# Three more seven-product couples in the down projections of a two-layer encoder kernel

## The chip, the cores and the metric

The kernel runs on one core of a Trainium2 chip. The metric is the device time of one launch in microseconds. Times of whole launches are medians over several runs. A profile is one execution of the program, recorded by the hardware profiler. TensorE (PE) multiplies, VectorE (DVE) and ScalarE (ACT) do the elementwise work, GpSimd (POOL) helps and issues some transfers, and SyncE (SP) issues most transfers to the DMA engines.

## What is computed

The reference is a trunk of two layers on a sequence of 256 tokens with 2048 features, in float32. Each layer adds a token mixer (bidirectional mLSTM in layer 0, bidirectional HGRN2 in layer 1) and then a convolutional gated MLP with 5504 hidden features. The change lies in the MLP, whose part of the reference is:

```python
def conv_glu(hn, w_up, conv_w, conv_b, w_down):
    u = hn @ w_up
    a, v = jnp.split(u, 2, axis=-1)
    s = a.shape[1]
    pad = CONV_W // 2
    ap = jnp.pad(a, ((0, 0), (pad, pad), (0, 0)))
    c = conv_b
    for j in range(CONV_W):
        c = c + ap[:, j:j + s] * conv_w[j]
    return (jax.nn.gelu(c, approximate=False) * v) @ w_down
...
    for layer in range(DEPTH):
        ...
        h = h + mix
        h = h + conv_glu(rmsnorm(h, norm_ffn_g[layer]), ffn_w_up[layer], ffn_conv_w[layer],
                         ffn_conv_b[layer], ffn_w_down[layer])
    return rmsnorm(h, final_g)
```

## The kernel before

**Precision.** Every float32 product is made of three matmuls. An operand is split into a high part, rounded by a copy to fp32r, and a low part, the rest. For weights ScalarE casts the high part `wh` (L147) and VectorE subtracts it from the original to get `wl` (L148). The three products are high by high, high by low and low by high (`product`, L236 issues their matmuls). Weights come from HBM as `raw` tiles, so the chain for each piece is load, cast, subtract, three matmuls.

**Stages.** The work of TensorE is one stream: mLSTM projections and chunks, its out projection, and then the MLP of layer 0; then the same for HGRN2 and the MLP of layer 1. The hidden features of an MLP are handled in two parts, 22 chunks of 128 in part 0 and 21 in part 1. Part 0's *up run* computes 22 chunks of a and v (L357 and L361, tokens on the columns), then its two *down pairs* multiply the 22 chunks into the four column blocks of 512 of the output, two blocks to a pair. Part 1 does the same with 21 chunks. The order of a whole MLP is thus: up run of part 0, two down pairs, up run of part 1, two down pairs.

**Eviction of an up chunk** (`done_up`, from L1197). ScalarE and VectorE add the two halves of the product (L1203, L1204), multiply by the norm's factor (L1206), do the convolution, the gelu and the gate (L1208 to L1212) in a temporary tile `avc`, and split the result into the tile `g` (L1214, L1215), which is the stationary operand of the down pair.

**A down pair** (`squares_by_seven`) takes the hidden chunks two at a time. Such a *couple*, or unit, is a 2 by 2 block product: two halves of the tokens by two hidden chunks, times two hidden chunks by two column blocks. Eight products of blocks do it, or seven in the manner of Strassen and Winograd, if sums of the blocks are there: S1 to S4 of the token blocks, T1 to T4 of the weight blocks. With three matmuls of 512 columns to a product, an ordinary unit has 24 matmuls and a unit by seven has 21. The products go to eight banks of PSUM: P1, P6, P7 and P5, which collect sums over all units by seven, and C11, C12, C21 and C22, which collect for the output blocks directly. After the last unit by seven, `mid` (L585 to L596) adds P1, P6, P7 and P5 into the hidden state `hm`; after the last unit of the pair, `done` (L602) adds the C banks. A following up chunk takes its two banks from the same ring as P1, P6, P7 and P5.

**Token sums** (`token_sums`, L565 to L579) are made during the up run: when the second chunk of a unit by seven is evicted, VectorE forms S1 to S4 (L571) and their splits (L572 to L576). Three of the four go to a new tile `sx`. The fourth is the last argument of the function; it overwrites halves of the tile `g` of the unit's first chunk that a unit by seven doesn't need.

**Weight sums.** Most of the units by seven have their T blocks prepared during an up run or a mixer (`prepare`, L638): the four blocks are loaded, four subtractions are made on VectorE, and the result is stored to a scratch tensor `tscr` in HBM. In the up runs the loads and stores are issued by GpSimd (L399). The down pair then loads a `raw` tile (1536 columns from the weights at L135, 512 from `tscr` at L199) and a `T` tile (1536 columns from `tscr`, L198). The units named in `FLY` make their T blocks on the spot instead (L207).

**Buffers.** `temporary` (L183) gives out the tiles `avc`, `T` and the f tiles. In the MLP they share one ring of three buffers (`TEMP`). Which units go by seven is set by the table `SEVEN`, by layer and part, the same units for both pairs of a part. The order in which instructions stand on each engine is made by a scheduler from the program, and SyncE's loads wait in their order for the buffer that each overwrites.

Of the kernel before, what the change touches and what calls it, by code (L numbers as in the profile page):

```python
# [49 lines left out]
SEVEN = ((1, 2, 3, 4, 5, 6, 7, 8, 9), (1, 2, 3, 4, 5, 6, 7, 8)), ((1, 2, 3, 4, 5, 6, 7, 8, 9), (1, 2, 3, 4, 5, 6, 7))  # L50
# [16 lines left out]
def trunk_kernel(ctx, tc, xT, x_d, fg_d, pp_d, cst_d, w_gate, w_first, w_aq, w_ak, w_av, w_ao, w_aout, w_ao2,  # L67
# [12 lines left out]
    ones = keep.tile([P, T], F32, name="ones")  # L80
# [144 lines left out]
    def squares_by_seven(ch, fetch, ready):  # L225
# [47 lines left out]
        units, last = (ch.nk + 1) // 2, max(ch.seven)  # L273
        for u in range(units):
# [127 lines left out]
    class Norm:  # L402
# [52 lines left out]
        def spread(self):  # L455

            dg = ev.tile([P, T], F32, tag="dg", bufs=1, name="dg")
# [5 lines left out]
            self.R_ = ev.tile([P, T], F32, tag="R", bufs=2, name="R")  # L463
# [233 lines left out]
    def mlstm(norm, nxt):  # L697
# [59 lines left out]
        def gates(gs):  # L757
            with tc.tile_pool(name="gt", bufs=1) as gp:
# [25 lines left out]
                scan(B[f_, 128:256], ones[f_, 128:256], lf[f_, 128:256], 0.0, ALU.mult, ALU.add)  # L784
# [108 lines left out]
        for pr in range(AH // 2):  # L893
# [36 lines left out]
            def done_first(ps, done_v=done_v):  # L930
# [252 lines left out]
    def ffn(layer, norm, nxt):  # L1183
# [13 lines left out]
        def done_up(f, i, GT, SX, seven):  # L1197
            def go(ps):
# [25 lines left out]
        for part, (f0, nf) in enumerate(((0, FA), (FA, FB))):  # L1224
            GT, SX, todo, finished = [], {}, [], []
# [9 lines left out]
            for i in range(nf):  # L1235
                chunks.append(Chunk("fm", w_up[layer, f0 + i], KT, norm.x, done_up(f0 + i, i, GT, SX, SEVEN[layer][part]),
# [17 lines left out]
            seven, fly = SEVEN[layer][part], FLY[2 * layer + part]  # L1254
            n = len(seven) - len(fly)
# [135 lines left out]
```

## Time and profile before

| what | value |
|---|---|
| median of 3 runs | 2366.11 us (2365.32 to 2366.84) |
| the profiled execution | 2365.95 us, with a span of 2364.2 us |
| granted TensorE clock | 1.00 in every MLP stage |
| TensorE busy | 2354.3 us |
| VectorE, ScalarE, GpSimd busy | 1995.5, 1469.7, 297.2 us |
| DMA | 632.98 MB, mean 268 GB/s |
| layer 0: up run 0, down pairs 0, up run 1, down pairs 1 begin at | 389, 634.6, 743.0, 976 us |
| layer 1: the same | 1665, 1910.7, 2018.2, 2251 us |
| layer 1's out projection begins at | 1597 us |

A row of the timeline gives the start in us, the duration, the engine, the line of the kernel, the operation, the output and input tiles, the shape, and in brackets how long the engine had been idle and what ended that. A group row gives the number of instructions, the busy time, the mean in ns of one, and the idle time ahead of them with the releasers. A row of the windows gives for a stretch of time the busy time of each engine, the granted clock, the share of the DMA engines and the rate. SPq is SyncE's queue, whose rows are the issues of transfers.

### The profile page before, as it was taken

The page shows a single profiled execution, that of the slowest core. Times are in us where ns is not written, and L with a number is a line of the kernel's source. Part 1 is how long each engine was busy: PE and PEld are TensorE (multiplying, and loading weights), DVE is VectorE, ACT ScalarE, POOL GpSimd, SP SyncE. Part 2 cuts the span into 40 slices and gives each one's busy share as a digit, 9 for nine tenths or more (in the row PEclk, how much of TensorE's full clock was granted, in tenths as well). Part 3 has the DMA queues.
Part 4 walks back from the last instruction along what each step waited for, and adds up shares of the span by engine and source line. Part 5 has one row for each costly group of instructions (what it writes and reads, how often), then busy time and mean ns, then how long its engine had stood idle before and what let it go on. Part 6 is the DMA issues. An engine that isn't in the chain of part 4 may idle for free.

```text
span 2364.2 us, 38476 instructions
## 1 busy us (share of the span) xinstructions
PE 2354.3 (100%) x14545; PEld 2017.3 (85%) x14545; DVE 1995.5 (84%) x3087; ACT 1469.7 (62%) x2340; POOL 297.2 (13%) x436
## 2 busy tenths in 40 slices
PE   9999999999999999999999999999999999999998
PEld 8888888888888888888888888888888888888887
DVE  7777687889898899897888888778799989899887
ACT  7655456555665555676777777766555566555565
POOL 0100001111000111000232322220011100111100
PEclk9999999999999999999999999999999999999999
DMA  8776656889788898796656666556788888799895
GB/s 302 240 245 244 214 193 217 289 312 320 251 324 320 310 323 317 267 330 227 214 200 224 218 216 213 202 174 235 250 306 318 297 299 330 278 326 328 279 356 201
DMA packets 122267, 632.98 MB, mean 268 GB/s; under 512 B 13776, under 2 KB 14928, under 8 KB 77664
## 3 DMA queue, kind: packets, MB, share of 16 engines
q1 hardware_dynamic: 92736, 525.83, 63.6%
q0 software_dynamic: 28768, 103.89, 12.1%
q8 instruction: 114, 1.87, 0.3%
q10 hardware_dynamic: 576, 0.79, 0.1%
q14 instruction: 73, 0.60, 0.1%
HBM read 562.24 MB, written 68.22 MB: 267 GB/s over the span
## 4 chain that ended last, share of the span: by engine, by line
PE 97%; DVE 1%; DMA 1%; issue 1%; ACT 0%; POOL 0%; SPq 0%; POOLq 0%; DVEq 0%; ACTq 0%
PE mm L357 37%; PE mm L361 19%; PE mm L373 18%; PE pc L236 11%; PE mm L236 7%; DVE wl L148 1%; PE pn L857 1%; PE py L1116 1%; PE pd L1066 0%; PE pa L1066 0%; DMA T<-tscr 0%; PE pz L438 0%; DMA raw<-in_w_first 0%; PE S L843 0%; ACT wh L147 0%
## 5 line engine op out<-in xcount | busy, mean ns | idle before, releaser
L357 PE MATMUL mm<-xt,wh 128*128 128x512 f32 x3776 | 1312.4, 394 | 0.0
L148 DVE TENSOR_TENSOR wl<-raw,wh 128x1024 fp32r<-128x1024 f32 (+1 forms) x844 | 1037.2, 1234 | 245.9 <-ACT wh L147 239.0
L147 ACT CAST wh<-raw 128x1024 fp32r<-128x1024 f32 (+1 forms) x844 | 876.3, 1043 | 545.3 <-PE mm L357 334.6
L361 PE MATMUL mm<-xt,wl 128*128 128x256 f32 x3776 | 1043.6, 278 | 0.0
L357 PEld LDWEIGHTS mm<-xt,wh 128*128 128x128 f32 x3776 | 705.7, 188 | 160.8 <-ACT jk L540 0.4
L361 PEld LDWEIGHTS mm<-xt,wl 128*128 128x128 f32 x3776 | 709.5, 188 | 4.5
L373 PE MATMUL mm<-wh,xt 128*128 128x512 f32 x1024 | 324.9, 393 | 0.5 <-ACT wh L147 0.3
L236 PE MATMUL pc<-wh,g 128*128 128x512 f32 (+1 forms) x716 | 243.2, 388 | 0.0
L373 PEld LDWEIGHTS mm<-wh,xt 128*128 128x128 f32 x1024 | 191.7, 188 | 40.0 <-ACT wh L147 1.0
L373 PE MATMUL mm<-wl,xt 128*128 128x512 f32 x512 | 199.7, 391 | 0.0
L638 DVE TENSOR_TENSOR praw<-praw 128x512 f32<-128x512 f32 x252 | 174.1, 691 | 12.9 <-DMA praw<-in_w_d 7.9
L236 PEld LDWEIGHTS pc<-wh,g 128*128 128x128 f32 x716 | 134.2, 188 | 28.0 <-ACT wh L147 0.4
L236 PE MATMUL mm<-wh,sx 128*128 128x512 f32 x432 | 153.6, 389 | 0.0
L148 DVE TENSOR_TENSOR wl<-T,wh 128x1024 fp32r<-128x1024 f32 (+1 forms) x144 | 136.4, 959 | 16.9 <-ACT wh L147 16.1
L147 ACT CAST wh<-T 128x1024 fp32r<-128x1024 f32 (+1 forms) x144 | 118.8, 834 | 49.4 <-DMA T<-tscr 19.5
L236 PE MATMUL pc<-wl,g 128*128 128x512 f32 (+1 forms) x358 | 138.8, 388 | 0.0
L1203 ACT COPY avc<-mm 128x256 f32<-128x256 f32 x172 | 64.3, 374 | 92.4 <-PE mm L361 92.4
L373 PEld LDWEIGHTS mm<-wl,xt 128*128 128x128 f32 x512 | 96.2, 188 | 18.5
L399 POOL DMA_DIRECT2D tscr<-praw x96 | 51.5, 537 | 468.0 <-DVE praw L638 446.9
L1079 DVE TENSOR_TENSOR QK<-QK,G 128x256 f32<-128x256 f32 x224 | 104.3, 514 | 6.2 <-ACT kq L1058 5.9
L1058 ACT COPY kq<-QK 128x512 f32<-128x512 f32 x112 | 74.4, 669 | 37.5 <-DVE QK L1079 29.6
L236 PEld LDWEIGHTS mm<-wh,sx 128*128 128x128 f32 x432 | 81.1, 188 | 16.8
(248 smaller groups left out, 2325.6 us busy)
## 6 DMA issues: line engine op xcount, KB each, us to landing
raw<-in_w_up SPq DMA_DIRECT2D x172, 1024.0 KB, 6.8
praw<-in_w_d POOLq DMA_DIRECT2D x96, 512.0 KB, 6.5
tscr<-praw POOLq DMA_DIRECT2D x96, 512.0 KB, 6.3
raw<-in_w_bq SPq DMA_DIRECT2D x48, 1024.0 KB, 5.0
T<-tscr SPq DMA_DIRECT2D x63, 768.0 KB, 7.8
raw<-in_w_d SPq DMA_DIRECT2D x60, 768.0 KB, 6.2
raw<-in_w_ao SPq DMA_DIRECT2D x24, 1024.0 KB, 4.9
raw<-in_w_d SPq DMA_DIRECT2D x24, 1024.0 KB, 6.9
```

The source lines that it names most:

```text
L147: pin(act.copy(wh[:, :m], r))
L148: pin(dve.tensor_tensor(wl[:, :m], r, wh[:, :m].bitcast(F32), ALU.subtract))
L236: pin(pe.matmul(ps, a, b, start=bank not in begun, stop=stop and i == 2))
L357: hold(pe.matmul(ps[f], wh[:, c:c + P], x, start=k + kk == 0, stop=False))
L361: hold(pe.matmul(ps[f][:, 0:T], wl[:, c:c + P], x[:, 0:T], start=False, stop=k + kk == ch.nk - 1))
L373: pe.matmul(ps[t], x[:, a + t * P:a + (t + 1) * P], w[:, c], start=st and i == 0, stop=sp and i == 2)
L399: tc.keep_in_program_order(pool.dma_start(dst, src))
L638: hold(dve.tensor_tensor(out, x, y, ALU.subtract))
L857: pe.matmul(pn[:, 0:258], w, v, start=(i == 0), stop=(i == len(parts) - 1))
L1058: act.copy(m, blocks(QK, h))
L1079: dve.tensor_tensor(two[:, j], two[:, j], by[:, j], ALU.mult)
L1203: act.copy(z, p[:, T:2 * T])
```

## The change

The table of units by seven now has one entry for each pair, not one for each part. Unit 10, the last of part 0, goes by seven in the second pair of both layers; it stands directly ahead of the up run of part 1. Unit 8 goes by seven in the first pair of part 1 of layer 1, the last pair but one of the kernel. That makes three more units by seven.

- A unit that goes by seven in one pair of its part only must leave both halves of `g` as they are for the other pair. Its fourth token sum goes to a tile of its own, `sy`.
- If the last unit of a pair goes by seven, its products into P1, P6, P7 and P5 come first, then `mid`, and then those into C12, C11 and C21. C22 gets its last product from the last unit that doesn't go by seven (`alone`).
- Three more units have their T blocks prepared: 12 more transfers on GpSimd's queue, three more T loads and three more loads from `tscr` on SyncE's, and 12 more subtractions at L638.
- To make room, the tile `ones` has 128 columns in place of 256, `dg` takes the buffer of `jk`, `R` has one buffer in place of two, and `gs` moves to a buffer of the MLP's pool.

```diff
-SEVEN = ((1, 2, 3, 4, 5, 6, 7, 8, 9), (1, 2, 3, 4, 5, 6, 7, 8)), ((1, 2, 3, 4, 5, 6, 7, 8, 9), (1, 2, 3, 4, 5, 6, 7))
+SEVEN = (range(1, 10), range(1, 11)), (range(1, 9), range(1, 9)), (range(1, 10), range(1, 11)), (range(1, 9), range(1, 8))
...
-    ones = keep.tile([P, T], F32, name="ones")
+    ones = keep.tile([P, P], F32, name="ones")
...
         units, last = (ch.nk + 1) // 2, max(ch.seven)
+        alone = max(set(range(units)) - set(ch.seven))
...
-                    product(ps, x, w, u == last and ps in psm_)
+                    product(ps, x, w, u == last if ps in psm_ else end)
...
-                products((P1, A11, B11), (C12, S4, B22))
+                products((P1, A11, B11))
+                if not end:
+                    products((C12, S4, B22))
                 T2, T3 = piece()
                 products((P6, S2, T2), (P7, S3, T3))
                 B21, T1 = piece()
-                products((C11, A12, B21), (P5, S1, T1))
+                if not end:
+                    products((C11, A12, B21))
+                products((P5, S1, T1))
                 T4, _ = piece()
-                products((C21, A22, T4))
+                if not end:
+                    products((C21, A22, T4))
                 if u == last:
                     ch.mid(psm_)
                     ch.rest = ch.ends
+                if end:
+                    products((C12, S4, B22), (C11, A12, B21), (C21, A22, T4))
                 continue
...
-                product(ps, y, v, end)
+                product(ps, y, v, end or ps is C22 and u == alone)
...
-            dg = ev.tile([P, T], F32, tag="dg", bufs=1, name="dg")
+            dg = ev.tile([P, 512], F32, tag="jk", bufs=1, name="dg")[:, 0:T]
...
-            self.R_ = ev.tile([P, T], F32, tag="R", bufs=2, name="R")
+            self.R_ = ev.tile([P, T], F32, tag="R", bufs=1, name="R")
...
-                gs = ev.tile([P, T], F32, tag="gs", name="gs")
-                act.copy(gs, pq[:, 0:T])
                 startup.close()
                 begin()
+                gs = box["mp"].tile([P, 768], F32, tag="W", bufs=2, name="gs")[:, 0:T]
+                act.copy(gs, pq[:, 0:T])
...
-                if i % 2 and i // 2 in seven:
-                    n = seven.index(i // 2)
+                if i % 2 and (i // 2 in seven or i // 2 in other):
+                    n = i // 2 - 1
                     z = GT[i - 1][:, P:T], GT[i - 1][:, T + P:2 * T]
+                    if not (i // 2 in seven and i // 2 in other):
+                        y = mp.tile([P, T], F32R, tag="sy", name="sy")
+                        z = y[:, 0:P], y[:, P:T]
                     SX[i // 2] = token_sums(mp, n, box["c"], c, avc[:, 0:2 * T], z)
```

**What moves.** The first place is SyncE's queue at the first pair of part 0 in layer 0. The `raw` tiles are those of units 3 onward (in_w_d0 is the pair's weights), the `T` tiles likewise: T_6409 before and T_6429 after belong to unit 3, T_6451 and T_6471 to unit 4. Before:

```order
162 L135 DMA raw_6407<-in_w_d0 128x1536
163 L199 DMA raw_6407<-tscr 128x512
164 L135 DMA raw_6449<-in_w_d0 128x1536
165 L199 DMA raw_6449<-tscr 128x512
166 L198 DMA T_6409<-tscr 128x1536
167 L135 DMA raw_6491<-in_w_d0 128x1536
168 L199 DMA raw_6491<-tscr 128x512
169 L198 DMA T_6451<-tscr 128x1536
170 L198 DMA T_6493<-tscr 128x1536
```

After, the same stretch of the queue:

```order
162 L135 DMA raw_6427<-in_w_d0 128x1536
163 L199 DMA raw_6427<-tscr 128x512
164 L135 DMA raw_6469<-in_w_d0 128x1536
165 L199 DMA raw_6469<-tscr 128x512
166 L135 DMA raw_6511<-in_w_d0 128x1536
167 L199 DMA raw_6511<-tscr 128x512
168 L198 DMA T_6429<-tscr 128x1536
169 L198 DMA T_6471<-tscr 128x1536
170 L198 DMA T_6513<-tscr 128x1536
```

The T of unit 3 has moved behind the raw tile of unit 5. In the ring of three it takes the buffer that unit 2's T lets go; before it took that of the last up chunk but one.

The second place is VectorE at the border from the second pair of part 0 to the up run of part 1 in layer 1. The hm and u rows are the evacuation of the banks named mm and pc; the wl rows from raw_20706 on (before) and from raw_20771 on (after) belong to the up run. Before:

```order
2446 L589 TENSOR_TENSOR hm_75<-hm_75,mm_20296 128x512
2447 L590 TENSOR_TENSOR u_20715<-u_20715,mm_20297 128x512
2448 L148 TENSOR_TENSOR wl_20697<-raw_20684,wh_20696 128x1024
2449 L591 TENSOR_TENSOR hm_75<-hm_75,mm_20299 128x512
2450 L593 TENSOR_TENSOR hm_75<-hm_75,mm_20299 128x512
2451 L148 TENSOR_TENSOR wl_20709<-raw_20706,wh_20708 128x1024
2452 L148 TENSOR_TENSOR wl_20726<-raw_20706,wh_20725 128x1024
```

After (mm_20347 is P5's bank, mm_20344 P1's):

```order
2469 L148 TENSOR_TENSOR wl_20765<-T_20734,wh_20764 128x512
2470 L148 TENSOR_TENSOR wl_20774<-raw_20771,wh_20773 128x1024
2471 L148 TENSOR_TENSOR wl_20784<-raw_20771,wh_20783 128x1024
2472 L148 TENSOR_TENSOR wl_20793<-raw_20790,wh_20792 128x1024
2473 L599 TENSOR_TENSOR hm_75<-hm_75,mm_20347 128x512
2474 L601 TENSOR_TENSOR hm_75<-hm_75,mm_20347 128x512
2475 L597 TENSOR_TENSOR hm_75<-hm_75,mm_20344 128x512
```

The reads of P1 and P5 stood ahead of the up run's first wl; now they stand behind three of them. (Lines above 271 are up to 8 higher in the changed kernel: L589 is L597, L591 is L599, L593 is L601.)

The third place is VectorE where layer 1's out projection begins. The f rows are token sums, yb the last head's output of HGRN2, hm the eviction of the projection's first column block. Before:

```order
1930 L148 TENSOR_TENSOR wl_16823<-raw_16784,wh_16822 128x1024
1931 L571 TENSOR_TENSOR f_16883<-f_16883 128x128
1932 L571 TENSOR_TENSOR f_16841<-f_16841 128x128
1933 L148 TENSOR_TENSOR wl_16874<-raw_16826,wh_16873 128x1024
1934 L554 TENSOR_TENSOR hm_75<-hm_75,mm_16533 128x512
1935 L554 TENSOR_TENSOR hm_75<-hm_75,mm_16534 128x512
```

After:

```order
1941 L148 TENSOR_TENSOR wl_16860<-raw_16854,wh_16859 128x1024
1942 L579 TENSOR_TENSOR f_16911<-f_16911 128x128
1943 L579 TENSOR_TENSOR f_16869<-f_16869 128x128
1944 L562 TENSOR_TENSOR hm_75<-hm_75,mm_16561 128x512
1945 L562 TENSOR_TENSOR hm_75<-hm_75,mm_16562 128x512
1946 L579 TENSOR_TENSOR f_16911<-f_16911 128x128
1947 L579 TENSOR_TENSOR f_16869<-f_16869 128x128
1948 L148 TENSOR_TENSOR wl_16851<-raw_16812,wh_16850 128x1024
```

The second wl of the stretch now stands behind two hm rows and two more sums.

More of the change, by code (lines that the diff above doesn't have):

```diff
@@ L1253, in ffn @@
             w0, w1 = w_d0[layer][:, f0 * 1024:(f0 + nf) * 1024], w_d3[layer] if part else w_d1[layer]
-            seven, fly = SEVEN[layer][part], FLY[2 * layer + part]
-            n = len(seven) - len(fly)
-            chunks.append(two(w0, 0, nxt if part else None, seven, fly, (0, 0, n) if part else (FIRST, n - FIRST)))
-            chunks.append(two(w1, 2, nxt if part and not ending else None, seven, fly, SPLIT[layer] if part else (0, n)))
+            fly = FLY[2 * layer + part]
+            m, n = (len(set(seven) - set(fly)) for seven in sevens)
+            chunks.append(two(w0, 0, nxt if part else None, sevens[0], fly, (0, 0, m) if part else (FIRST, m - FIRST)))
+            chunks.append(two(w1, 2, nxt if part and not ending else None, sevens[1], fly, SPLIT[layer] if part else (0, n)))
             if part:
@@ L1371, in build @@
     mscr = nc.dram_tensor("mscr", (64, T), F32, kind="Internal").ap()
-    tscr = nc.dram_tensor("tscr", (len(SEVEN_MIX) + 2 * sum(len(s) for layer in SEVEN for s in layer), P, 2048), F32, kind="Internal").ap()
+    tscr = nc.dram_tensor("tscr", (len(SEVEN_MIX) + sum(len(s) for pairs in SEVEN for s in pairs), P, 2048), F32, kind="Internal").ap()
     with tile.TileContext(nc, schedule_with_timeline_sim=True) as tc:
```

8 lines of the change are left out of this document (4 added, 4 removed).

## The prediction

> **What bounds the kernel now.** I read the page's shares first, then the chain of waits, then the table of windows for the feed-forward stages, and last the timelines around the places where the order of the changed program differs.
>
> ```profile
> PE 2354.3 (100%) x14545; PEld 2017.3 (85%) x14545; DVE 1995.5 (84%) x3087; ACT 1469.7 (62%) x2340; POOL 297.2 (13%) x436
> ...
> PE 97%; DVE 1%; DMA 1%; issue 1%; ACT 0%; POOL 0%; SPq 0%; POOLq 0%; DVEq 0%; ACTq 0%
> ```
>
> TensorE is busy for 2354.3 of 2364.2 us and carries 97% of the chain. A matmul that goes away is therefore worth its full pace, as long as the work that feeds TensorE still arrives in time. How much room that work has is read stage by stage (up run of layer 0, down pairs of part 0 in layers 0 and 1, down pairs of part 1 in layer 1):
>
> ```profile
> core 0: us, PE busy (x) PEld busy (x) DVE busy (x) ACT busy (x) POOL busy (x), PEclk, DMA share, GB/s
> 389.00:634.00 245.00, 245.00 (x1418) 214.32 (x1417) 214.23 (x349) 140.47 (x222) 26.39 (x49) 1.00 0.84 294
> 634.00:743.00 109.00, 108.66 (x479) 89.36 (x478) 100.06 (x112) 72.94 (x86) 3.53 (x2) 1.00 0.86 319
> ...
> 1910.00:2018.00 108.00, 108.00 (x480) 89.48 (x479) 99.83 (x113) 72.72 (x86) 3.54 (x2) 1.00 0.87 322
> ...
> 2251.00:2356.00 105.00, 105.00 (x479) 87.54 (x477) 90.83 (x110) 68.71 (x87) 5.69 (x5) 1.00 0.76 285
> ```
>
> TensorE has no gap anywhere, but in the down pairs VectorE is busy for 100.06 of 109 us (0.92) and the DMA engines for 0.86 at 319 GB/s. Nothing there has much slack, so a buffer that comes free a few microseconds later, or an evacuation that now falls on a border, can show. The granted clock is 1.00 throughout.
>
> **The matmuls that go.** A couple by seven products has 21 matmuls of 512 columns instead of 24. The chain gives their pace:
>
> ```profile
> 2289.62 14.05 PE pc L236 x62
> ```
>
> 14.05 / 62 = 0.2266 us. Three couples save 9 matmuls: 9 x 0.2266 = **-2.04 us**, all on the path. In the section "Back-to-back issue gap" of "TensorE: Matmul & The Clock Gate", the Trainium skill puts two warm matmuls of 512 columns 216 ns apart; by that the nine would be worth 1.94 us. The row above has 227 ns, and the measurement decides.
>
> **T of unit 3 in the first pair of part 0, layer 0.** Buffers of the tag avc (three) serve the up chunks' evictions and the T tiles alike. Before, SyncE loaded the T of unit 3 early, as soon as up chunk 20 had let its buffer go, and the T of unit 4 when the T of unit 2 was used up:
>
> ```profile
> 636.77 0.33 SPq L198 DMA_DIRECT2D T<-tscr  x1
> 644.54 0.33 SPq L135 DMA_DIRECT2D raw<-in_w_d  x1
> 644.92 0.43 SPq L199 DMA_DIRECT2D raw<-tscr  x1
> 645.39 3.37 SPq L198 DMA_DIRECT2D T<-tscr  x3
> ```
>
> Now chunk 21, the last of the up run, makes token sums for unit 10 out of chunk 20's and 21's values, and holds both buffers. The order of SyncE shows the early T gone: T of unit 3 stands after the raw of unit 5, where T of unit 4 stood, and waits for the same release. So its time is that of the old T of unit 4:
>
> ```profile
> 645.31 1.05 ACT L147 CAST wh<-T 128x1024 fp32r<-128x1024 f32 x1
> ...
> 652.01 1.05 ACT L147 CAST wh<-T 128x1024 fp32r<-128x1024 f32 x1 [1.61 <-DMA T<-tscr]
> ```
>
> The first row is the old cast of unit 3's T, the second that of unit 4's, which ScalarE started as the data landed (it had idled 1.61 us for it): 645.39 to 652.01 is 6.6 us. TensorE begins the pair here:
>
> ```profile
> 634.61 0.39 PE L236 MATMUL pc<-wh,g 128*128 128x512 f32 x1
> ```
>
> By the order of TensorE, the first product with unit 3's T is the 73rd matmul of the pair: 634.61 + 72 x 0.2266 = 650.93. The cast ends at 652.01 + 1.05 = 653.06, or up to 0.5 later, since token sums (0.2 us each) now stand ahead of the release on VectorE. That is a wait of 2.1 to 2.6 us. Then wl, 1.23 us on VectorE:
>
> ```profile
> L148 DVE TENSOR_TENSOR wl<-T,wh 128x1024 fp32r<-128x1024 f32 x72 | 88.9, 1234 | 15.7 <-ACT wh L147 15.3
> L148 DVE TENSOR_TENSOR wl<-T,wh 128x512 fp32r<-128x512 f32 x72 | 49.2, 683 | 1.2 <-ACT wh L147 0.9
> ```
>
> TensorE has three or four matmuls (0.7 to 0.9 us) that need only wh, so some 0.5 us of the wl shows as well. I take **+2.9** (2.0 to 3.4).
>
> **The same in layer 1.** There T of unit 4 was issued at 1921.99 and cast at 1928.96:
>
> ```profile
> 1914.69 0.33 SPq L198 DMA_DIRECT2D T<-tscr  x1
> ...
> 1921.99 3.01 SPq L198 DMA_DIRECT2D T<-tscr  x2
> ```
> ```profile
> 1928.96 1.05 ACT L147 CAST wh<-T 128x1024 fp32r<-128x1024 f32 x1 [2.41 <-DMA T<-tscr]
> ```
> ```profile
> 1910.72 0.39 PE L236 MATMUL pc<-wh,g 128*128 128x512 f32 x1
> ```
>
> Here the product is the 79th: 1910.72 + 78 x 0.2266 = 1928.40, against 1928.96 + 1.05 = 1930.01. That is 1.6, and again about 0.5 for wl, less 0.1 for leeway: **+2.0** (1.0 to 3.0). What comes behind, the T of units 4 and 5, is issued as before and has the whole stall as new leeway.
>
> **Evacuation at the border to the up run of part 1.** (Lines of the changed kernel are 8 higher from here on: L589 to L602 become L597 to L610, L554 becomes L562.) Before, the sums P1, P6, P7, P5 ended with unit 9, and their evacuation (L588 to L596) lay beside unit 10's 24 matmuls (5.44 us). Now they end with unit 10, and the next up chunk's first two matmuls go into the banks of P5 and P1. The durations are those of before:
>
> ```profile
> 2013.24 0.68 DVE L593 TENSOR_TENSOR hm<-hm,mm 128x512 f32<-128x512 f32 x1
> 2013.84 2.35 DVE L148 TENSOR_TENSOR wl<-raw,wh 128x1024 fp32r<-128x1024 f32 x2
> 2016.11 0.68 DVE L592 TENSOR_TENSOR hm<-hm,u 128x512 f32<-128x512 f32 x1
> 2016.71 0.68 DVE L602 TENSOR_TENSOR hm<-hm,pc 128x512 f32<-128x512 f32 x1
> ```
>
> An evacuation takes 0.60 from start to start (2016.11 to 2016.71) and 0.68 to its end, a wl half of 2.35. In layer 1 the new order has three wl of the up run ahead of the two reads of P5 (L599, L601). The cast for the last of them waits for a buffer that TensorE frees seven matmuls, 1.59 us, before the run: 1.05 + 1.17 + 0.60 + 0.68 = 3.50, so the first up matmul waits 1.9, and the second about 0.4 more for P1's read. A first cast that finds its buffer earlier would leave about 1.2 in all. I take **+1.8** (1.2 to 2.4). In layer 0 the order is P5 (two reads), one wl, P1. P5 ends 11 matmuls (2.49 us) ahead of the run; 0.60 + 0.60 + 1.17 + 0.68 = 3.05 after it P1's bank is free, for the second up matmul: **+0.55** (0.2 to 0.9).
>
> **The border into layer 1's out pair.** The order of VectorE changes there too. Two hm additions (L562) and two sums move ahead of a wl that TensorE needs 27 matmuls after the last transpose of hgrn:
>
> ```profile
> 1601.25 0.27 PE L1137 MATMUL pz<-ident,y 128*128 128x128 f32 x1
> ```
> ```profile
> 1601.56 1.43 DVE L681 TENSOR_TENSOR f<-yb 128x256 f32<-128x256 f32 x4 [2.94 <-PE pz L1137]
> ...
> 1603.90 1.22 DVE L148 TENSOR_TENSOR wl<-raw,wh 128x1024 fp32r<-128x1024 f32 x1
> 1605.04 0.49 DVE L571 TENSOR_TENSOR f<-f 128x128 f32<-128x128 f32 x2
> 1605.44 1.22 DVE L148 TENSOR_TENSOR wl<-raw,wh 128x1024 fp32r<-128x1024 f32 x1
> 1606.58 1.28 DVE L554 TENSOR_TENSOR hm<-hm,mm 128x512 f32<-128x512 f32 x2
> ```
>
> VectorE has no gap from 1601.56 on. Up to 1605.44 nothing changes; then two hm (1.19), two sums (0.40), and the wl: it ends at 1605.44 + 1.19 + 0.40 + 1.22 = 1608.25. TensorE is there at 1601.3 + 27 x 0.2266 = 1607.4: **+0.8** (0 to 1.0).
>
> **Work that is added beside.** Each new couple adds a preparation in the up run (four subtractions, two 512 KB loads and two stores on GpSimd's queue) and token sums:
>
> ```profile
> L638 DVE TENSOR_TENSOR praw<-praw 128x512 f32<-128x512 f32 x252 | 174.1, 691 | 12.9 <-DMA praw<-in_w_d 7.9
> ```
>
> 4 x 0.69 = 2.8 us a couple, with the sums (some 2 us) 4.8 on VectorE, whose share in the up run goes from 0.874 to 0.89, and 2 MB more for the DMA engines, 7 us at 294 GB/s, from 0.84 to 0.87. Neither fills up: I cost it at nothing, and if that cover were gone, each couple would cost its 4.8 us. In the pairs each new couple adds two wl on VectorE (1.23 + 0.68), and 0.79 MB of reads. One place there is tight already:
>
> ```profile
> 690.63 0.39 PE L236 MATMUL mm<-wh,sx 128*128 128x512 f32 x1
> 691.33 0.50 PE L236 MATMUL mm<-wl,sx 128*128 128x512 f32 x1 [0.32 <-DVE wl L148]
> ```
>
> From 690.63 to 691.33 is 0.70 where 0.23 is the pace: TensorE waits 0.47 for wl at the border of layer 0's pairs. For such places in the pairs with a new couple I add **+0.5** (-0.9, if the old ones vanish, to +2.5). Unit 8 in the first pair of layer 1's part 1 has only this cost, as its VectorE share is 90.83 of 105. The smaller ones constant, dg and R in one buffer each and gs in another pool cost nothing: the values are read before the next is written in any case.
>
> **The sum.** -2.04 + 2.9 + 2.0 + 1.8 + 0.55 + 0.8 + 0.5 = +6.5 us. The profiled execution took 2365.95 us (span 2364.2), 0.16 under the median of 2366.11, so the two can stand for each other: 2366.0 + 6.5 = **2372.5**, 0.27% slower. 0.2%, 4.7 us, is about what a measurement of this kernel can tell from no change. With all terms at their low ends together it would be +1.5, at their high ends +11.2; since they are independent I take 2369.5 to 2375.5 as the forecast's own range.
>
> **Rivals.** First, *the T of unit 3 lands quickly*. The 6.6 us are those of a queue with other transfers in it. The page's list of transfers has quicker ones:
>
> ```profile
> T<-tscr SPq DMA_DIRECT2D x63, 768.0 KB, 7.8
> ...
> raw<-in_w_aout SPq DMA_DIRECT2D x8, 1024.0 KB, 4.7
> ```
>
> At 4.7 us, T would be there at 650.09 and cast by 651.14 (0.2 late), and in layer 1 by 1927.74, in time: 4.7 us of the sum go, 2372.5 - 4.7 = 2367.8, no change. The section "The DMA setup-cost knee" of "SBUF — State Buffer" in the Trainium skill fits a transfer with 2 us plus its bytes over 436 GB/s, 3.8 us for 768 KB; by that rule both stalls go. The row of 7.8 us disagrees, and the 1 MB of raw issued 0.85 us ahead is against it: 15%.
>
> Second, *everything hides, and the nine matmuls are all*: 2366.0 - 2.0 = 2364.0, within 0.2%, the not slower side. It decides if VectorE takes P5 and P1 in time and chunk 21's sums release the buffers sooner than their order says. For it speaks that the trace has hardly a stall now; against it the fixed orders. 10%. More than about 3 us (the 2.04 and the old 0.9) can't be gained, so faster by over 0.2% is left 3% for what I don't see.
>
> Third, *the DMA engines become the bound in the pairs with new couples*. Each new couple adds 0.79 MB, 2.4 us at the 322 GB/s of the window, while TensorE gets 0.68 shorter. It decides if the loads that wait behind the late T never catch up; two of three pairs then grow by 2.4 each: 2372.5 + 4.9 = 2377.4. For it speak the shares of 0.86 and 0.87 and the 7.8 us; against it that ScalarE waited only 1.61 and 2.41 for a T. 17%.
>
> **The numbers.** Forecast 55%, quick T 15%, all hidden 10%, DMA-bound 17%, others 3%. Slower by over 0.2% (above 2370.8) are the third rival and seven eighths of the forecast: 65%. Within are the rest of the forecast and the first two rivals: 32%; faster 3%. The range of 8 in 10 goes from 2365.5, which leaves out most of "all hidden", to 2377.0.
>
> **What would show it.** In the profile after, TensorE should wait near 651 us for wh from T for 2 to 2.6, and near 1931 for 1.5; SyncE should issue the first T of a group only after 645. The first up matmuls of both parts 1 should start late by 0.5 and 2 us, waiting for VectorE's L601 and L597. Near 1611 a wait for wl of 0.8. The count of matmuls should be nine lower at L236. If TensorE's rows run on without a gap near 651, the main term is wrong; if gaps sit in many couples of one pair, the third rival is right.

## The result, and the profile after

The changed kernel takes 2381.03 us (median of 6 runs, 2375.25 to 2389.06) against 2366.35 of before (6 runs, 2365.32 to 2367.35): the ratio is 1.0064, with a 95% interval of 1.0046 to 1.0082. It is slower, as forecast, but by 14.7 us and not by 6.5, and outside the range. The runs of this one program also lie 14 us apart, where those of before lay within 2.

The profiled execution took 2382.35 us, with a span of 2380.6: 16.4 more than the profile of before. The page after:

```profile
PE 2360.7 (99%) x14536; PEld 2016.8 (85%) x14536; DVE 2009.9 (84%) x3123; ACT 1475.8 (62%) x2352; POOL 305.6 (13%) x448
...
PE 94%; DVE 3%; DMA 2%; issue 1%; ACT 1%; POOL 0%; SPq 0%; POOLq 0%; DVEq 0%; ACTq 0%
```

TensorE has nine matmuls fewer (14536) and yet is busy for 6.4 us more. Waits alone don't do that: somewhere it multiplies more slowly. The starts of the stages, read from TensorE's timeline in both traces, say where the 16.4 us went:

| stage | before | after | more |
|---|---|---|---|
| up to the up run of layer 0 | 389.03 | 389.73 | +0.70 |
| up run 0, layer 0 | 245.58 | 245.52 | -0.06 |
| down pairs 0, layer 0 | 108.42 | 111.54 | +3.12 |
| up run 1, layer 0 | 232.96 | 238.09 | **+5.13** |
| down pairs 1, layer 0 | 105.79 | 105.69 | -0.10 |
| HGRN2 | 515.71 | 516.60 | +0.89 |
| out projection, layer 1 | 67.65 | 68.62 | +0.97 |
| up run 0, layer 1 | 245.58 | 245.52 | -0.06 |
| down pairs 0, layer 1 | 107.46 | 111.13 | +3.67 |
| up run 1, layer 1 | 232.96 | 233.35 | +0.39 |
| down pairs 1, layer 1 | 105.08 | 106.71 | +1.63 |

(The two border waits of layer 1 lie one in the row of down pairs 0, 0.9, and one in the row of up run 1.)

**The forecast waits are there.** SyncE's queue at the first pair of layer 0, then ScalarE, then TensorE:

```profile
645.76 0.43 SPq L199 DMA_DIRECT2D raw<-tscr  x1
646.28 1.90 SPq L198 DMA_DIRECT2D T<-tscr  x2
```
```profile
652.73 1.04 ACT L147 CAST wh<-T 128x1024 fp32r<-128x1024 f32 x1 [4.15 <-DMA T<-tscr]
```
```profile
651.37 0.39 PE L236 MATMUL pc<-wh,g 128*128 128x512 f32 x1
653.83 0.73 PE L236 MATMUL mm<-wh,sx 128*128 128x512 f32 x2 [2.07 <-ACT wh L147]
654.78 0.50 PE L236 MATMUL pc<-wh,g 128*128 128x512 f32 x1 [0.22 <-ACT wh L147]
...
655.81 0.63 PE L236 MATMUL mm<-wl,sx 128*128 128x512 f32 x1
656.23 0.63 PE L236 MATMUL mm<-wh,sx 128*128 128x512 f32 x1
...
658.79 0.59 PE L236 MATMUL mm<-wl,sx 128*128 128x512 f32 x1
659.22 0.40 PE L236 MATMUL mm<-wh,sx 128*128 128x512 f32 x1
```

The T of unit 3 is issued after 645 us, 0.9 later than before's T of unit 4, and TensorE waits 2.07 and 0.22 us. Then comes something that the forecast did not have: from 655.81 to 659.22 a matmul of 512 columns follows the last after 0.427 us and not 0.2266. The granted clock is 0.66 in the window around it, which is half the clock for 3.4 of its 5 us:

```profile
655.00:660.00 5.00, 5.00 (x16) 3.95 (x16) 5.00 (x6) 3.95 (x6) 0.00 (x0) 0.66 0.70 225
```

Eight matmuls at half the clock cost 8 x 0.2 = 1.6 us on top of the wait.

**The border to the up run of layer 0**, TensorE and VectorE:

```profile
746.79 0.39 PE L365 MATMUL mm<-xt,wh 128*128 128x512 f32 x1
747.57 0.50 PE L365 MATMUL mm<-xt,wh 128*128 128x512 f32 x1 [0.39 <-DVE hm L597]
```
```profile
745.10 0.68 DVE L601 TENSOR_TENSOR hm<-hm,mm 128x512 f32<-128x512 f32 x1
745.70 1.22 DVE L148 TENSOR_TENSOR wl<-raw,wh 128x1024 fp32r<-128x1024 f32 x1
746.84 0.68 DVE L597 TENSOR_TENSOR hm<-hm,mm 128x512 f32<-128x512 f32 x1
```

The second up matmul starts 0.78 after the first where the pace is 0.23: 0.55 us late, for P1's bank, behind P5's reads and one wl. That is the forecast's figure, in part by luck, as told below. But the run that it opens is longer by 4.6 us more than that. Its start and end, before and after:

```profile
743.03 0.62 PE L357 MATMUL mm<-xt,wh 128*128 128x512 f32 x2
...
975.99 0.40 PE L236 MATMUL pc<-wh,g 128*128 128x512 f32 x1
```
```profile
984.76 0.28 PE L369 MATMUL mm<-xt,wl 128*128 128x256 f32 x1
984.88 0.40 PE L236 MATMUL pc<-wh,g 128*128 128x512 f32 x1
```

Before: 975.99 - 743.03 = 232.96 us for 672 pairs of a 512 and a 256 column matmul, 0.3467 us each. After: 984.88 - 746.79 - 0.55 = 237.54, 0.3535 each. In the table of windows the whole run shows no gap but the 0.39 us above, no lower clock, and no more DMA than the run before had. Before, then after:

```profile
743.00:976.00 233.00, 233.00 (x1346) 203.74 (x1345) 205.71 (x326) 129.08 (x202) 29.17 (x50) 1.00 0.86 302
746.00:984.00 238.00, 237.61 (x1344) 205.75 (x1343) 210.26 (x331) 129.21 (x202) 29.23 (x50) 1.00 0.86 300
```

From start to start, pair after pair, the trace repeats 0.232 + 0.118, 0.240 + 0.120, 0.236 + 0.114 there, and 0.233 + 0.117, 0.231 + 0.113, 0.232 + 0.118 in the same run before. It is a second steady pace, 2% slower, held for 238 us. Up run 1 of layer 1 has the good pace, 0.3467, in this trace.

**The other waits**: at the out pair, at layer 1's border, and at the border to the last pair.

```profile
1616.73 0.61 PE L236 MATMUL pc<-wh,yb 128*128 128x512 f32 x2
1617.99 0.50 PE L236 MATMUL pc<-wl,yb 128*128 128x512 f32 x1 [0.65 <-DVE wl L148]
```
```profile
2031.31 0.39 PE L236 MATMUL pc<-wh,g 128*128 128x512 f32 x1
2032.44 1.01 PE L365 MATMUL mm<-xt,wh 128*128 128x512 f32 x2 [0.75 <-ACT wh L147]
```
```profile
2317.48 0.39 PE L236 MATMUL pc<-wh,g 128*128 128x512 f32 x1
2319.71 0.47 PE L236 MATMUL pc<-wh,g 128*128 128x512 f32 x1 [1.84 <-DVE hm L610]
```

From start to start, less the pace, they are 0.81, 0.91 (and 0.28 for the second up matmul), and 2.0. At layer 1's border the profile names a cast that ended at 2032.33. VectorE's second read of P5 ended almost with it, at 2032.30, and P1's read at 2032.89:

```profile
2031.02 0.68 DVE L599 TENSOR_TENSOR hm<-hm,mm 128x512 f32<-128x512 f32 x1
2031.62 0.68 DVE L601 TENSOR_TENSOR hm<-hm,mm 128x512 f32<-128x512 f32 x1
2032.21 0.68 DVE L597 TENSOR_TENSOR hm<-hm,mm 128x512 f32<-128x512 f32 x1
```

I read the wait as one for P5's bank: in layer 0 the like cast (746.99 to 748.04) ended after the run had begun. No run separates the two.

### The profile page after: what moved, and what is told of

Read it like the earlier page. It is cut to its first block, busy times and chain, and to the rows that moved or that the text cites. A ratio compares the mean times of both kernels' runs of the same rounds, so it can differ in the third digit from the quotient of the medians.

```text
span 2380.6 us, 38547 instructions
## 1 busy us (share of the span) xinstructions
PE 2360.7 (99%) x14536; PEld 2016.8 (85%) x14536; DVE 2009.9 (84%) x3123; ACT 1475.8 (62%) x2352; POOL 305.6 (13%) x448
## 4 chain that ended last, share of the span: by engine, by line
PE 94%; DVE 3%; DMA 2%; issue 1%; ACT 1%; POOL 0%; SPq 0%; POOLq 0%; DVEq 0%; ACTq 0%
PE mm L365 37%; PE mm L369 18%; PE mm L381 18%; PE pc L236 9%; PE mm L236 7%; DVE wl L148 1%; DMA T<-tscr 1%; PE pn L865 1%; PE py L1124 1%; ACT wh L147 1%; DMA raw<-in_w_d 1%; PE pd L1074 0%; PE pz L446 0%; PE pa L1074 0%; DMA raw<-in_w_first 0%
## 5 line engine op out<-in xcount | busy, mean ns | idle before, releaser
L236 PE MATMUL pc<-wh,g 128*128 128x512 f32 (+1 forms) x680 | 233.7, 390 | 2.1 <-DVE hm L610 1.8
L646 DVE TENSOR_TENSOR praw<-praw 128x512 f32<-128x512 f32 x264 | 182.3, 691 | 12.9 <-DMA praw<-in_w_d 7.7
L148 DVE TENSOR_TENSOR wl<-T,wh 128x512 fp32r<-128x512 f32 (+1 forms) x150 | 142.8, 967 | 27.3 <-ACT wh L147 26.6
L236 PE MATMUL mm<-wh,sx 128*128 128x512 f32 x450 | 160.2, 390 | 2.7 <-ACT wh L147 2.7
L147 ACT CAST wh<-T 128x512 fp32r<-128x512 f32 (+1 forms) x150 | 123.2, 835 | 63.9 <-DMA T<-tscr 26.9
L236 PEld LDWEIGHTS pc<-wh,g 128*128 128x128 f32 x680 | 127.8, 188 | 30.2 <-issue 2.2
L236 PE MATMUL pc<-wl,g 128*128 128x512 f32 (+1 forms) x340 | 132.3, 389 | 0.8 <-DVE wl L148 0.8
```

What stands on the lines that cost most here:

```text
L147: pin(act.copy(wh[:, :m], r))
L148: pin(dve.tensor_tensor(wl[:, :m], r, wh[:, :m].bitcast(F32), ALU.subtract))
L236: pin(pe.matmul(ps, a, b, start=bank not in begun, stop=stop and i == 2))
L646: hold(dve.tensor_tensor(out, x, y, ALU.subtract))
```

## The experiments

The theories, as the expectations name them. **A**: the loss beyond the waits is TensorE running more slowly by itself, an up run in the slow pace of 0.3533 us a pair (0.3467 is the good one), which comes or not by chance when the run starts after a wait (the pace is *drawn*), and half the clock after a wait of over 2 us. **B**: the work added beside the up run slows it (ports, DMA). **C**: the smaller buffers cost. Later **A2**: the pace is fixed by how the first matmuls of a run follow each other, by their order or by a wait among them. **D**: only waits draw the pace. **E**: working bank by bank, or the loads beside, slows it.

**again**, the changed kernel once more.

> The changed kernel once more, for a second trace and a spread of times. Theory A (the loss beyond the forecast is TensorE running slower by itself: a phase in which a pair of a 512 and a 256 column matmul takes 0.3533 us in place of 0.3467, entered by chance of how an up run starts after a wait, and a half clock after a wait of over 2 us) expects times that scatter by 5 to 14 us, and a trace in which the waits (T of unit 3 near 651 us 2.2, near 1939 us 1.3; banks 0.55 and 1.2; out pair 0.8; last pair but one 2.0) are the same within 0.3 us, while the slow pace may be in another up run, or in none. Theory B (the up run of part 1 in layer 0 is slowed by the added work beside it, on ports or DMA) expects the slow pace in just that up run again, and the same time within 1 us.

2384.12 us (2378.82 to 2384.88, 5 runs). The trace has the same waits (2.34 and 0.39 near 651 us, then seven matmuls of 0.427; 0.55; 0.80; 0.96 and 0.46; 0.91 and 0.28), the last border 0.58 in place of 2.0. But now both up runs of part 1 are slow. The one of layer 1, whose border wait is the same as in the first trace:

```profile
2031.22 1.01 PE L365 MATMUL mm<-xt,wh 128*128 128x512 f32 x2 [0.75 <-ACT wh L147]
...
2269.03 0.40 PE L236 MATMUL pc<-wh,g 128*128 128x512 f32 x1
```

237.81 us, against 233.35 in the first trace (2032.44 to 2265.79). The same program, the same wait, another pace: B, with the same place slow each time, doesn't explain that.

**memory_only**, the new code and buffers with the old table.

```diff
-SEVEN = (range(1, 10), range(1, 11)), (range(1, 9), range(1, 9)), (range(1, 10), range(1, 11)), (range(1, 9), range(1, 8))
+SEVEN = (range(1, 10), range(1, 10)), (range(1, 9), range(1, 9)), (range(1, 10), range(1, 10)), (range(1, 8), range(1, 8))
```

> The changed program with the old table: units 1 to 9, 1 to 8, 1 to 9, 1 to 7 for both pairs of a part, so no unit is new and only the smaller buffers, the moved gs and the new code remain. Theory A expects no wait at the out pair of layer 1 (the order there is that of before again) and the time of before, 2366 us within 1.5. Rival C (the smaller buffers or the moved gs cost by themselves, as R and dg in one buffer each) expects 1 us or more above before, at the starts of the stages that norm them.

2365.44 us (11 runs, 2364.33 to 2366.96), ratio to before 1.0000 (0.9992 to 1.0009). No wait at the out pair. C falls; all of the loss comes with the units.

**unit8_only**, the old table but for unit 8 in the last pair but one (`range(1, 9), range(1, 8)` for part 1 of layer 1).

> Of the three new units only unit 8 in the first pair of part 1 in layer 1. Theory A expects -0.68 for three matmuls and a wait at the border to the last pair of about 2.0 us where the added evacuation (L602 to L604) and two wl stand ahead of the C banks' eviction: 2366.3 + 1.3 = 2367.6, and no waits at 651, 747, 1939 or 2032 us. If the 2 us come only from the lateness that the earlier stages hand on, that border has no wait and the time is 2365.7.

2366.24 us (11 runs, 2365.39 to 2367.77), ratio 1.0002 (0.9993 to 1.0010). The border has only a small wait, for wl and not for a bank:

```profile
2302.84 0.39 PE L236 MATMUL mm<-wh,sx 128*128 128x512 f32 x1
2303.41 0.50 PE L236 MATMUL mm<-wl,sx 128*128 128x512 f32 x1 [0.18 <-DVE wl L148]
```

From start to start that is 0.34 us late, and there is another 0.2 some 41 us on. So the 2.0 us there (0.58 in *again*) come with what the earlier stages hand on and not with unit 8 alone. The unit's three matmuls are still not gained.

**own_c**, all three units, but chunk 20's values no longer hold an avc buffer.

```diff
                 a, v, c = (avc[:, j * T:(j + 1) * T] for j in range(3))
+                if i == 20 and 10 in other and 10 not in seven:
+                    c = ev.tile([P, 512], F32, tag="jk", bufs=1, name="own")[:, 0:T]
```

> The changed kernel with one edit: the values of up chunk 20 are kept in the buffer of jk and not in its avc, so its avc is free as before and the T of unit 3 is loaded early again. Theory A expects the waits near 651 us (2.2 + 0.4) and near 1939 us (0.8 + 0.5) gone, and with the first the half clock behind it (about 1.8 us): some 5 us less than the changed kernel when both are in the good phase, the waits at the borders 747 and 2032 us, the out pair and the last border left; 2371 to 2376 us. If the waits had another cause than the buffer (a DMA queue that is simply full) they stay.

2375.17 us (8 runs, 2366.22 to 2381.64). In the trace both T waits are gone and TensorE runs through the place where it had waited:

```profile
651.01 0.39 PE L236 MATMUL mm<-wl,g 128*128 128x512 f32 x1
651.23 0.39 PE L236 MATMUL mm<-wh,g 128*128 128x512 f32 x1
```

So the buffer was the cause, and with the wait the half clock went. This trace is of the fastest run (2366.22, span 2364.4). It has the border waits of the first trace (0.55; 0.91 and 0.28) and the out pair's 0.80, but both up runs in the good pace: from 742.02 to 975.64, 233.62 with its wait of 0.55. The other runs lie from 4.9 to 15.4 us above it, outside the 2371 to 2376 expected on both sides. The two border waits cost 1.7 us themselves, here as in both traces of the changed kernel; what is behind them is worth more. Two up runs in the slow pace would make 9.2 of the 15.4; no trace shows the rest.

**held_banks**, the old units, and a wait made on purpose: five small VectorE instructions (their results unused) keep the four banks until C11 is complete. `hold` is set for the second pair of part 0 alone.

```diff
+        if ch.hold:
+            u = ev.tile([P, T], F32, tag="hold", bufs=1, name="hold")
+            dve.tensor_tensor(u[:, 0:P], C11[:, 0:P], ident, ALU.mult)
+            for p in psm_:
+                dve.tensor_tensor(u[:, P:2 * P], p[:, 0:P], u[:, 0:P], ALU.mult)
         held.pop()
         ch.done(psa_)
```

> The kernel of memory_only (the old units, no new work beside anything), with five small VectorE instructions at the end of the second pair of part 0 that read the banks of P1, P6, P7 and P5 once more, after C11 is complete, so that the next up run has to wait for its banks. Their results are not used. Theory A (TensorE's pace in an up run is drawn anew when the run starts after a wait; over 2 us of waiting brings a half clock) expects, beside the waits at the two borders (1 to 4 us each), up runs of part 1 at 0.3533 us a pair in some executions, +4.6 us for each, so times that scatter over 5 us or more, and a stretch of matmuls at 0.427 us behind a wait of over 2 us. Theory B (the added preparation and loads slow the up run) expects 0.3467 us a pair in the trace, and times above before by the waits alone, with a scatter of 2 us as before.

2383.74 us; the runs are 2378.81, 2383.51, 2383.74, 2387.46 and 2387.76. The profiled one is the lowest and has both up runs in the good pace, so the slow pace itself isn't in a trace here; the other four lie 4.7, 4.9, 8.7 and 9.0 us above it, once and twice the 4.6 us of a slow up run. There is no other added work, so B doesn't explain the scatter; whether it is the slow pace or more of the half clock isn't shown. The half clock is in the trace, with waits of 2.42 and 1.30 us. The clock of 0.86 in the first window is half the clock for the last 1.5 us of it, so it began within 0.3 us of the end of the first wait; the second window has half throughout:

```profile
742.81 0.39 PE L236 MATMUL pc<-wh,g 128*128 128x512 f32 x1
745.62 0.53 PE L370 MATMUL mm<-xt,wh 128*128 128x512 f32 x1 [2.42 <-DVE hold L333]
747.45 0.80 PE L370 MATMUL mm<-xt,wh 128*128 128x512 f32 x1 [1.30 <-DVE hold L333]
```
```profile
742.00:747.40 5.40, 1.73 (x7) 0.84 (x5) 5.40 (x10) 1.04 (x1) 2.56 (x2) 0.86 0.59 194
747.40:752.60 5.20, 5.15 (x16) 4.48 (x17) 1.68 (x4) 0.27 (x1) 3.01 (x5) 0.50 0.83 276
```

In layer 1 the wait was 3.58 us, and half the clock came there too.

**first_f**, own_c with the first weight piece of the run bank by bank, so that P1's bank is asked for 1.4 us later. **first_f_L0** is the same with unit 10 of layer 0 as the only new unit.

```diff
+                    if ch.swap == (0, 2) and k == 0:
+                        ops = [(kk, f, part) for f in range(2) for kk in range(n) for part in "hl"]
                     hold = pin if ch.fixed else lambda ins: ins
```

> own_c with the first weight piece of the up run of part 1 in another order: eight matmuls into its first bank, then eight into its second. In layer 0 the second bank (P1's) is then asked for 1.4 us later. Theory A expects the wait of 0.55 us at layer 0's border gone and with it the draw: that up run always at 0.3467 us a pair; in layer 1 the first bank's wait of 0.9 stays, and the draw with it. So times in two groups 4.6 us apart, the lower at 2365 to 2366, the median at or below own_c's 2375. Theory B expects the scatter of own_c unchanged, 2366 to 2382.

> first_f with only one of the three new units, unit 10 in layer 0. No wait should be left at a border to an up run. Theory A expects the good pace in all up runs and the scatter of before (2 us): -0.68 for three matmuls, +0.8 if the out pair's order is that of the changed kernel, so 2365.0 to 2366.2. Theory B expects the up run of part 1 in layer 0 slow at least in some executions, since the work beside it is that of the changed kernel there: 2369 or more in some.

2374.43 us (2370.96 to 2377.81) and 2375.20 (2373.20 to 2377.22), 5 runs each. Layer 0's border wait is gone in both traces, but for 0.07 us, and yet the run behind it is slow in both: 979.63 - 742.14 = 237.5 and 979.40 - 741.91 = 237.5. The times are those that B expected, but in first_f_L0 layer 1's run is slow as well (237.4), which has no wait and none of the new work. In first_f layer 1's run starts in the same order behind a wait of 0.91, and there it has the good pace (2256.72 - 2023.68 = 233.04). The edit had also undone the two exchanges of the old order, by which the run began with two of 512 and two of 256. So A falls in its first form: a wait isn't needed for the slow pace. This led to A2.

**before_noswap**, the kernel before without those exchanges, and nothing else.

```diff
-                                    swap=(0, 2) if part and i == 0 else (3,) if f0 + i == 1 else (), paced=True,
+                                    swap=() if part and i == 0 else (3,) if f0 + i == 1 else (), paced=True,
```

> The kernel before, with one edit: the first chunk of the up run of part 1 has its matmuls in the plain order (512, 256, 512, 256) from the start, without the two exchanges that begin it with two of 512 and two of 256 twice. No work is added and no wait. Theory A2 (the pace of an up run, 0.3467 or 0.3533 us a pair, is fixed by how its first matmuls follow each other: by their order, or by where a wait falls among them; load beside it plays no part) expects both up runs of part 1 in one pace throughout, and that it can be the slow one: 2366 if the plain order enters the good pace, 2370.7 if one run and 2375.3 if both are slow, with the small scatter of before, as nothing waits. Theory B (load) expects 2366. A third theory D, that only waits draw the pace, expects 2366 too.

2374.83 us, all 5 runs within 0.75 (2374.28 to 2375.03): ratio 1.0035 (1.0023 to 1.0048). Both runs are slow in the trace; that of layer 0:

```profile
743.17 0.39 PE L357 MATMUL mm<-xt,wh 128*128 128x512 f32 x1
743.40 0.28 PE L361 MATMUL mm<-xt,wl 128*128 128x256 f32 x1
...
980.61 0.40 PE L236 MATMUL pc<-wh,g 128*128 128x512 f32 x1
```

980.61 - 743.17 = 237.44, 4.5 us more than with the exchanges. No wait, no added work, no wider scatter: two exchanges among the first eight matmuls of each run decide over 8.6 us. D falls, and what B blames isn't needed for the slow pace.

**steered**, first_f_L0 with the exchanges moved to the second piece (places 8 and 10).

```diff
-                    if ch.swap == (0, 2) and k == 0:
+                    if ch.swap == (8, 10) and k == 0:
...
-                                    swap=(0, 2) if part and i == 0 else (3,) if f0 + i == 1 else (), paced=True,
+                                    swap=(8, 10) if part and i == 0 else (3,) if f0 + i == 1 else (), paced=True,
```

> first_f_L0 with the two exchanges put at the start of the second weight piece of that chunk (places 8 and 10 in place of 0 and 2), so that the first piece is bank by bank as there and what follows begins as in the kernel before. Units: only unit 10 in layer 0 is new. Theory A2 expects that the exchanges, not the bank order, set the pace: both up runs of part 1 at 0.3467 us a pair in the trace, where first_f_L0 had 0.3533 in both, and with no wait at either border a time of first_f_L0's trace less 2 x 4.5: 2365 to 2367 with the small scatter of before. Theory B expects the up run of part 1 in layer 0 slow again, 2370 or more.

2376.62 us (2374.75 to 2377.46). Both runs are slow, 237.5 and 237.4. That expectation was wrong: exchanges made later, after eight pairs by turns, don't lead back to the good pace.

**sized_L0**, first_f_L0 with the bank order set ahead of the exchanges, so that the first eight matmuls have the old sizes (512, 512, 256, 256 twice), all into the first bank. **sized** is the same with all three units.

> first_f_L0 (only unit 10 in layer 0 is new, its avc kept free, the first piece bank by bank), but with the sizes of the first eight matmuls in the order of the kernel before: 512, 512, 256, 256 twice, all into the first bank. No wait is left at either border. Theory A2, made sharper (the pace of an up run is fixed by the sequence of sizes in its first matmuls and by waits among them; banks, tiles and load play no part) expects 0.3467 us a pair in both up runs of part 1 and so 2375.2 of first_f_L0 less 2 x 4.4: 2365.5 to 2367, with a scatter of 2 us. Theory E (working bank by bank, or the loads beside, is what slows it) expects 2373 to 2377 as first_f_L0 and steered.

> The same with all three new units. In layer 1 the wait of 0.9 us ahead of the first up matmul is left (VectorE's reads of P5 stand behind three wl). Theory A2 expects layer 0's up run always at 0.3467 us a pair, and layer 1's drawn by that wait: own_c's three groups become two, about 2366 and 2371, nothing above 2373. If layer 0's is drawn all the same, times up to 2376 and more come up as with own_c.

sized_L0: 2366.55 us (11 runs, 2365.05 to 2369.63), ratio 1.0008 (0.9999 to 1.0017). Both runs are in the good pace, that of layer 0 with the same work beside it as in first_f_L0:

```profile
741.59 0.61 PE L367 MATMUL mm<-xt,wh 128*128 128x512 f32 x2
742.04 0.40 PE L371 MATMUL mm<-xt,wl 128*128 128x256 f32 x2
...
974.55 0.40 PE L236 MATMUL pc<-wh,g 128*128 128x512 f32 x1
```

974.55 - 741.59 = 232.96, the number of before. B and E fall: banks and work are those of first_f_L0, only the sizes of eight matmuls changed places, and each of the two runs is 4.5 us shorter. sized: 2370.49 us (2369.13 to 2378.81, 6 runs); in its trace layer 0's run is good (232.95) and layer 1's, which still starts after a wait of 0.91, is slow (237.50). Five runs lie between 2369 and 2373 and none at 2366; the sixth, 2378.81, is above what was expected, and no trace shows why.

**grouped**, the kernel before with each weight piece of the paced chunks sorted by size, eight of 512 and then eight of 256.

```diff
-                    for i in ch.swap:
+                    if ch.paced:
+                        ops.sort(key=lambda o: o[2] == "l")
+                    for i in () if ch.paced else ch.swap:
```

> The kernel before, with the matmuls of each weight piece in the paced chunks of 256 tokens (the up runs and part of HGRN2's projections) sorted by size: eight of 512 columns, then eight of 256, in place of 512 and 256 by turns. No work is added or left out. In the traces so far a 512 behind a 512 starts 0.2267 us after it and a 256 behind a 256 0.113, together 0.340, while by turns a pair takes 0.3467 or 0.3533. Theory A2 (the pace hangs on the sequence of sizes alone) expects a pace between 0.340 and 0.3467 a pair: with two changes of size in place of sixteen, up to 5 ns less for each of some 2750 pairs of the up runs, 2366 - 14 = 2352 at best, and between 2358 and 2366 if a change of size costs more when it is rarer. If the clock or the loads set the pace, 2366 as before.

2377.60 us (2376.63 to 2381.84), ratio 1.0051 (1.0037 to 1.0065). The expectation was wrong. Up run 1 of layer 0 takes 979.73 - 745.12 = 234.61, 0.3491 a pair: a third pace. The first eight of each kind take 1.82 and 0.95 us:

```profile
745.12 1.98 PE L359 MATMUL mm<-xt,wh 128*128 128x512 f32 x8
746.94 1.11 PE L363 MATMUL mm<-xt,wl 128*128 128x256 f32 x8
747.89 0.40 PE L359 MATMUL mm<-xt,wh 128*128 128x512 f32 x1
```

0.95 / 8 = 0.119 is what a 256 behind a 256 costs in a row, and not the 0.113 seen in single ones. HGRN2 brought waits of its own in this order, two of them (2.14 and 1.99 us) with half the clock behind them.

## Why the prediction was wrong

**What held.** The direction, and every wait that the sum names: each came where it was forecast. The T of unit 3 in layer 0: +2.9 forecast, 2.2 + 0.4 measured; *own_c* shows the buffer as the cause. In layer 1: +2.0, 0.84 + 0.46 measured, within the bounds. Layer 0's border +0.55, 0.55 measured, but the agreement is luck: what I had worked out, 3.05 - 2.49, was the time from the run's start to P1's release, and the second matmul's own 0.23 had still to come off. The release came 0.2 later than that (747.52, 0.72 after the start), and the two errors cancelled. Layer 1's +1.8, 0.91 + 0.28 measured: it is the case of the cast that finds its buffer earlier, for which I had given 1.2. VectorE began on P5's bank at 2031.02, 0.5 before TensorE came to the border. Out pair +0.8, 0.81. "Such places in the pairs with a new couple", +0.5: it was mis-sized. In the first trace they are 0.6, 0.5 and 0.2 in layer 1's second pair and 2.0 at the last border, while the old 0.5 and 0.2 in layer 0 have gone, in all some 2.6. That is the upper bound, but the 2.0 was 0.6 in the second trace. All six together are 9.1 against 8.55 in the sum; they agree because this one, 2.1 above, makes up for the others, which are 1.6 below.

**What failed** is a step that isn't a term of the sum. It charged each wait its own length and let all other matmuls go on at the pace of before; a change of that pace it put at nothing, with no reason but "The granted clock is 1.00 throughout" in the trace before. Two things don't stay. After a wait of 2.1 us TensorE ran at half the clock for 3.4 us (1.6 us lost). And up run 1 of layer 0 went at 0.3535 us a pair and not 0.3467, 4.6 us in the first trace; in the second the one of layer 1 did so too, for twice that. With these two the profile's 16.4 us add up: waits of 2.62, 1.30, 0.55, 1.19, 0.81 and 2.6, -2.04 for the matmuls, half clock 1.6, slow pace 4.6, and 0.70 and 0.89 that lie ahead of the MLP and in HGRN2: 14.8. The rest, 1.6, is a wait of 0.40 in layer 0's last pairs and some 1.1 in waits of under 0.2 each in the down pairs.

**The rivals.** The quick T didn't come: the cast began 6.5 us after its issue. All hidden didn't come either. The third rival, a DMA bound with 2377.4, is nearest to the time and was not the cause: the DMA share of the windows is 0.84 in the down pairs of layer 0's part 0, where 0.86 stood before, and removing the waits in *own_c* gave one run at 2366.2.

**What stays open.** What holds TensorE in one pace or the other isn't in the traces. That a wait redraws it is shown by the same wait with different paces in *after*, *again* and *own_c*; that the runs of one program differ mainly in this is argued, not shown. The five times of held_banks lie in steps of about 4.6 us; those of own_c and of the changed kernel spread evenly, and over more than two slow up runs explain. The 0.89 us in HGRN2, an idle time that the profile ascribes to nothing, comes and goes between traces. Why sized_L0 scatters over 4.6 us in 11 runs wasn't tried.

No version beats the kernel before: memory_only equals it, and the units by seven that were added cost as much in waits (sized_L0 0.8 at the out pair) as their matmuls save.

## What to carry to other kernels

When TensorE alternates between matmuls of two sizes, look at the time from start to start, not at the busy share or the granted clock: here there was more than one steady pace, and the first few matmuls of a stretch chose it. A short wait at the head of a long run, harmless by its length, then puts the whole run at stake, and times of one program that scatter more than before can be a sign of it. Before a couple or an eviction is moved to such a border, ask what the first matmul behind it waits for, and give it a bank that is long free while keeping the order of sizes.

## What the runs showed of the hardware that was not expected

- Matmuls of 512 and 256 columns by turns ran at 0.3467 or at 0.3533 us a pair over 1344 matmuls, and at 0.3491 in groups of eight. The order of the sizes of the first eight was enough to choose (sized_L0 against first_f_L0). With a wait of 0.55 us between the first and the second it came out either way (*after*, slow; *own_c*, good). The Trainium skill, in "Back-to-back issue gap" of "TensorE: Matmul & The Clock Gate", gives N / 2.4 + 2.5 ns as the warm gap of an isolated matmul, by which an estimate for such a pair is 216 + 109 = 325 ns. All traces here are above it.
- Waits of 2.07 us (*after*), 2.42 us (*held_banks*), 2.14 and 1.99 us (*grouped*) were followed by half the clock, with 0.427 us for 512 columns: in *after* 2.0 us behind the wait and for 3.4 us, in *held_banks* within 0.3 us of the first wait's end and for some 6.7, the second wait of 1.30 among them. A wait of 1.84 us at the last border of *after* was not. The Trainium skill, in "What's actually happening" of "TensorE: Matmul & The Clock Gate", puts the fall to half the clock after an idle window of about 3.4 us; here less was enough.
